# Four strips of array columns for the samples' state products, and PSUM banks of their own

## The chip, the cores and the metric

The kernel runs on one core of a Trainium2 chip. The metric is the device time of one execution in microseconds; the median of several runs is compared. A core has five engines with a queue each: TensorE (PE, with weight loads as PEld), VectorE (DVE), ScalarE (ACT), GpSimd (POOL) and SyncE (SP), which here issues most DMAs. Every queue is worked off in order.

## The reference, cut to what matters

One layer of a decoder trunk for a prompt of 1024 tokens and for eight samples of one token each (`NS = 8`), which share the weights: a combined input projection, gated DeltaNet heads, sliding-window attention, an output mix, and a gated feed-forward part. The change is in what the eight samples do with their carried DeltaNet states, one 128x128 state per sample and head (8 heads):

```python
def _gdn_recurrent(q, k, v, beta, g, S0):
    def step(S, inp):
        q_t, k_t, v_t, b_t, g_t = inp
        S = S * jnp.exp(g_t)[..., None, None]
        delta = (v_t - jnp.einsum('bhk,bhkv->bhv', k_t, S)) * b_t[..., None]
        S = S + jnp.einsum('bhk,bhv->bhkv', k_t, delta)
        return S, jnp.einsum('bhk,bhkv->bhv', q_t, S)
```

and in the stage of the two branches around it:

```python
y_a = _gdn_out(o_a, gdn_gate, lp['gdn_onorm_w']) @ lp['w_gdn_out']
y_b = o_b @ lp['w_swa_out']
mix = (jax.nn.sigmoid(ga) * y_a + jax.nn.sigmoid(gb) * y_b) @ lp['w_o']
```

## The kernel before

The program is one long straight line with stages: conditioning and attention; the DeltaNet heads of the prompt; the **branches**; the output mix, feed-forward part and final norm (`second_half`). The order of instructions on each engine is set when the program is built: each operation has a priority (the order of the Python code, shifted by hand in places), and a planner with a model of costs takes, for each engine, what is ready and has room first. On the chip each queue then keeps that order.

A projection (`project`, lines 152 to 164) multiplies 128 output channels by all 1032 columns (1024 of the prompt, 8 of the samples) in three parts of 384, 384 and 264 columns. Each part is 24 matmuls, three for each of eight slices of the contraction (lines 180 to 182: high half by high half, high by low, low by high), added up in one PSUM bank. `evac` empties the bank. `next_mm` (line 174) takes the PSUM pool of the next part from the list `self.mm` in turn. In the branches that list is `[pmm, pmm, pmf]`: pool `pmm` has two banks under the tag "mm", `pmf` one.

In `branches` the attention output ("b2h"/"b2l") is projected with w_swa_out, one tile of 128 channels after another; DVE empties each part by a product with a gate (line 1256) that a DMA reads back from memory into one of three buffers "sgx" (line 1300). Then the operand is replaced by the DeltaNet output "oa" (`load_part`, lines 1191 and 1192), projected with w_gdn_out, and the two are added and split into halves (lines 1260 to 1266).

Between these projection parts one step of `sample_delta` is emitted at a time, each ending at a `yield`. Its steps: load the eight states of each head (line 1079, on SP); activation; norms of q and k by a matmul against ones, a power on GpSimd, a diagonal on DVE and a spread back over the partitions (`rows_rsqrt`, line 1174, and `rows_spread`, line 1180); `kq` and the table "wide" (line 1104); dots of q and k (line 1109); **the products with the states** (line 1121), for two halves of four heads; a copy out of PSUM by ACT (line 1122); eight transposes (line 1126, recorded under the helper's line 190); the deltas; the output with a second norm; and the update of the states (GpSimd line 1161, DVE line 1163, stores line 1165). The samples' tiles in PSUM all come from `pmm`, tag "mm": they share the two banks with the projections.

"wide" holds, for each head, eight blocks of 16 columns, one for each sample b; block b is zero but for columns 2b and 2b + 1, where k and q of that sample stand. The eight products of a head are thus added up in the same 16 partitions of PSUM, row 2b and 2b + 1 being those of sample b. An f32 matmul is two passes on PE. The modulation (line 264), in the first stage, multiplies in a different way: four products, each with 32 columns of weights, write to partitions 0, 32, 64 and 96 onward, and a second product with "strips" (line 270), which holds four stacked identities, adds the four strips up.

Of the kernel before, what the change touches and what calls it, by code (L numbers as in the profile page):

```python
# [9 lines left out]
F32 = mybir.dt.float32  # L10
F32R = mybir.dt.float32r
# [4 lines left out]
PSUM = bass.MemoryType.PSUM  # L16
DRAM = bass.MemoryType.DRAM

P = 128
NP = 1024  # L20
NS = 8
NT = NP + NS
KC = 8
H = 8
# [16 lines left out]
def bc(ap, dim, n):  # L41

    a = ap.unsqueeze(dim)
    shape = list(a.shape)
    shape[dim] = n
    return a.broadcast_to(shape)


def carver(*rooms):

    used = [0] * len(rooms)

    def small(*shape, r=0):
        n = 1
        for x in shape:
            n *= x
        v = rooms[r][:, used[r]:used[r] + n]
        used[r] += n
        letters = "abcd"[:len(shape)]
        return v.rearrange(f"p ({' '.join(letters)}) -> p {' '.join(letters)}", **dict(zip(letters, shape)))  # L60

    return small


class Step:
# [1003 lines left out]
    def sample_delta(self):  # L1069

        nc, I = self.nc, self.I
        zl, cw = self.zl, self.cw
        a, b, c, d, e = (self.t(self.b1, [P, KC, PARTS[t][1]], f"b1{x}{t}", F32R).bitcast(F32).rearrange("p k n -> p (k n)")
                         for x, t in (("h", 1), ("l", 1), ("h", 2), ("l", 2), ("h", 0)))
        small = carver(d, e)
        S0 = []
        for h in range(H):
            S0.append((a, b, c)[h // 3][:, h % 3 * NP:h % 3 * NP + NP].rearrange("p (b v) -> p b v", b=NS))
            nc.sync.dma_start(S0[h], I["state_gdn_S"][0][:, h].rearrange("b k v -> k b v"))
        act, tmp = small(24, NS), small(24, NS)  # L1080
        nc.vector.tensor_tensor(act, zl[:, :, 3:11], bc(cw[:, 3, :], 2, NS), op=ALU.mult)
        nc.vector.tensor_tensor(act, act, self.gsp, op=ALU.add)
        nc.scalar.activation(tmp, act, AF.Tanh, scale=0.5)
        nc.vector.scalar_tensor_tensor(act, tmp, 1.0, act, op0=ALU.add, op1=ALU.mult)

        flat = lambda a: a.rearrange("p a h b -> p (a h b)")
        f3 = lambda a: a.rearrange("p h b -> p (h b)")
        qk = act[:, 0:16, :].rearrange("p (a h) b -> p a h b", a=2)
        v = act[:, 16:24, :]
        sq = small(2, H, NS)  # L1090
        nc.vector.tensor_tensor(sq, qk, qk, op=ALU.mult)
        wide = small(H, NS, 2 * NS)
        nc.gpsimd.memset(wide, 0.0)
        yield
        ps = self.t(self.pmm, [P, 1], "mm")
        nc.tensor.matmul(ps, flat(sq), self.ones[:, 0:1], start=True, stop=True)
        r = self.rows_rsqrt(small, ps, P, 1.0, 4 * EPS)
        yield
        rl = self.rows_spread(*r).rearrange("p (a h b) -> p a h b", a=2, h=H)
        kq = self.const([P, H, NS, 2], "kq")  # L1100
        nc.vector.tensor_tensor(kq[:, :, :, 0], qk[:, 1], rl[:, 1], op=ALU.mult)
        nc.vector.scalar_tensor_tensor(kq[:, :, :, 1], qk[:, 0], P ** -0.5, rl[:, 0], op0=ALU.mult, op1=ALU.mult)
        for i in range(2):
            nc.vector.tensor_copy(wide.rearrange("p h b c -> p h (b c)")[:, :, i::2 * NS + 2], kq[:, :, :, i])
        yield
        pr = small(H, NS)
        nc.vector.tensor_tensor(pr, kq[:, :, :, 0], kq[:, :, :, 1], op=ALU.mult)
        dots = self.t(self.pmm, [P, H, NS], "mm")
        nc.tensor.matmul(f3(dots), self.ones, f3(pr), start=True, stop=True)
        qkd = small(H, NS)  # L1110
        nc.vector.tensor_copy(qkd, dots)
        yield
        eg = self.egb[:, :, 0, :].rearrange("p b h -> p h b")
        beta = self.egb[:, :, 1, :].rearrange("p b h -> p h b")

        rows = small(H, P, r=1)[:2 * NS]
        for h0 in (0, 4):
            ps = self.t(self.pmm, [2 * NS, 4, P], "mm")
            for h in range(4):
                for b in range(NS):  # L1120
                    nc.tensor.matmul(ps[:, h, :], wide[:, h0 + h, b, :], S0[h0 + h][:, b, :], start=b == 0, stop=b == NS - 1)
            nc.scalar.copy(rows[:, h0:h0 + 4, :], ps)
            yield
        pks = self.t(self.pmm, [P, H, NS, 2], "mm")
        for h in range(H):
            self.transpose(pks[:, h].rearrange("p b a -> p (b a)"), rows[:, h, :])
        yield
        pk, dl, o = small(H, NS, 2), small(H, NS), small(H, NS)
        nc.vector.tensor_tensor(pk, pks, bc(eg, 3, 2), op=ALU.mult)
        nc.vector.tensor_scalar_mul(dl, v, 0.5)  # L1130
        nc.vector.tensor_tensor(dl, dl, pk[:, :, :, 0], op=ALU.subtract)
        nc.vector.tensor_tensor(dl, dl, beta, op=ALU.mult)
        yield
        ps = self.t(self.pmm, [H * NS, P], "mm")
        self.transpose(ps, f3(dl))
        dlT = small(P, r=1)[:H * NS]
        nc.vector.tensor_copy(dlT, ps)
        dlr = self.t(self.dr, [H, NS, P], "dlr")
        nc.sync.dma_start(dlr.rearrange("h b v -> (h b) v"), dlT)
        yield  # L1140
        nc.vector.tensor_tensor(o, qkd, dl, op=ALU.mult)
        nc.vector.tensor_tensor(o, o, pk[:, :, :, 1], op=ALU.add)

        nc.vector.tensor_tensor(pr, o, o, op=ALU.mult)
        yield
        ps = self.t(self.pmm, [H * NS, 1], "mm")
        nc.tensor.matmul(ps, f3(pr), self.ones[:, 0:1], start=True, stop=True)
        r = self.rows_rsqrt(small, ps, H * NS, 1.0 / P, EPS)
        yield
        rl = self.rows_spread(*r).rearrange("p (h b) -> p h b", h=H)  # L1150
        nc.vector.tensor_tensor(o, o, rl, op=ALU.mult)
        nc.vector.scalar_tensor_tensor(o, o, self.onw, self.sgs, op0=ALU.mult, op1=ALU.mult)
        nc.sync.dma_start(self.oa[:, :, NP:NT].rearrange("i p b -> p i b"), o)

        for h in range(H):
            if h % 4 == 0:
                yield
            db = self.t(self.b1, [P, KC, 384], "b1l0", F32R).bitcast(F32).rearrange("p k n -> p (k n)") if h == 0 else db
            d = db[:, h % 3 * NP:h % 3 * NP + NP].rearrange("p (b v) -> p b v", b=NS)
            nc.sync.dma_start(d, dlr[h].unsqueeze(0).broadcast_to([P, NS, P]))  # L1160
            nc.gpsimd.tensor_tensor(d, d, bc(kq[:, h, :, 0], 2, P), op=ALU.mult)
            for b in range(NS):
                nc.vector.scalar_tensor_tensor(S0[h][:, b, :], S0[h][:, b, :], self.egb[:, b, 0, h:h + 1], d[:, b, :],
                                               op0=ALU.mult, op1=ALU.add)
            nc.sync.dma_start(self.O[3][0][:, h].rearrange("b k v -> k b v"), S0[h])
# [10 lines left out]

    def rows_spread(self, dg, n):

        out = self.t(self.pmm, [P, n], "mm")
        self.nc.tensor.matmul(out, self.ones[:n, :], dg[:n, :n], start=True, stop=True)  # L1180
        return out

# [62 lines left out]
    def branches(self, pool, pool2):  # L1245
        nc, I = self.nc, self.I
# [3 lines left out]
        for _ in self.filler:  # L1250
            pass
        samples = self.sample_delta()
        gate = lambda src, j, t: self.gate_part(pool, src[j][:, PARTS[t][0]:PARTS[t][0] + PARTS[t][1]], t)

        def yb_out(t, ps):
# [536 lines left out]
    def run(self):  # L1792
        S, nc = ExitStack, self.nc
# [54 lines left out]
            self.a2 = self.norm_scale(self.const([P, KC, 9], "a2"), 32, self.n2w)  # L1848
        with S() as c:
            pool2, pool = self.pool("p6b", 1, ctx=c), self.pool("p6", 1, ctx=c)  # L1850
            self.branches(pool, pool2)
        cg.close()
        self.wctx.close()
        self.second_half()
# [40 lines left out]
```

## Time and profile before

| | |
|---|---|
| median of 3 runs | 2203.2 us (2201.71 to 2215.32) |
| the profiled execution | 2208.18 us, its span 2206.5 us |
| PE busy / weight loads | 2116.8 us (96%) / 1997.0 us |
| DVE, ACT, POOL busy | 1350.5, 792.4, 298.9 us |
| mean granted clock of PE | 0.967 |

Busy time counts from the start to the modelled end of an instruction, and matmuls overlap, so the length of a block of matmuls is better read from start to start. A clock of 1.00 is full speed. An instruction's line is the line of the kernel at which it was recorded; instructions of a helper carry the helper's line. A releaser is the instruction whose semaphore ended an engine's wait.

### The profile page before, as it was taken

The numbers are of one execution on the slowest core, as the hardware profiler recorded it, in microseconds if no ns is written. First come the engines' busy times: TensorE is split into PE (matmuls) and PEld (weight loads), VectorE is DVE, ScalarE is ACT, GpSimd is POOL, SyncE is SP. The second block draws the span as 40 slices with busy tenths as digits, with TensorE's granted clock in tenths as the row PEclk, the third lists the DMA queues.
The fourth block names the chain that finished last, engine by engine and source line by source line (L and its number), as shares of the span: only waits on it lengthen the run. The fifth ranks groups of instructions, "written<-read, shape, count | busy, mean of one in ns | idle before, by whom it ended". The sixth has DMA issues, their size and how long they took to land.

```text
span 2206.5 us, 41136 instructions
## 1 busy us (share of the span) xinstructions
PE 2116.8 (96%) x16507; PEld 1997.0 (91%) x16507; DVE 1350.5 (61%) x2935; ACT 792.4 (36%) x2010; POOL 298.9 (14%) x395
## 2 busy tenths in 40 slices
PE   7899998999999999999999899999999999999998
PEld 3886876899899998998998899999999999999998
DVE  5756665365555756765323665578776776766565
ACT  3445454333243434334222032344333433432102
POOL 1000000011221210111111300002332332100000
PEclk9999997999999989999999999999999999999999
DMA  9333231142222321221327663622323232363202
GB/s 345 108 107 113 86 129 60 49 132 63 70 79 59 80 64 42 62 65 50 88 75 209 202 188 103 184 64 78 97 73 92 69 96 68 97 220 126 87 3 78
DMA packets 265090, 223.93 MB, mean 101 GB/s; under 512 B 57462, under 2 KB 232473, under 8 KB 264882
## 3 DMA queue, kind: packets, MB, share of 16 engines
q1 hardware_dynamic: 263570, 217.01, 32.3%
q10 hardware_dynamic: 1152, 3.70, 0.4%
q8 instruction: 130, 2.13, 0.4%
q14 instruction: 62, 0.51, 0.1%
q0 software_dynamic: 176, 0.59, 0.1%
HBM read 171.28 MB, written 52.35 MB: 101 GB/s over the span
## 4 chain that ended last, share of the span: by engine, by line
PE 82%; DVE 7%; DMA 5%; ACT 3%; issue 2%; SPq 1%; POOL 1%; DVEq 0%; POOLq 0%; ACTq 0%
PE mm L180 18%; PE mm L182 17%; PE mm L181 17%; PE wv L181 3%; PE wv L182 3%; PE wv L180 3%; PE wy L182 2%; PE wy L180 2%; PE wy L181 2%; PE pt L190 1%; PE pv L648 1%; PE tp L190 1%; PE pv L646 1%; PE mm L264 1%; DMA raw<-in_w_in_dram 1%
## 5 line engine op out<-in xcount | busy, mean ns | idle before, releaser
L180 PE MATMUL mm<-b1h,wh 128*128 128x384 f32 (+1 forms) x1440 | 474.4, 331 | 13.6 <-DVE kl L540 4.7
L181 PE MATMUL mm<-b1l,wh 128*128 128x384 f32 (+1 forms) x1440 | 468.3, 326 | 0.0
L182 PE MATMUL mm<-b1h,wl 128*128 128x384 f32 (+1 forms) x1440 | 466.6, 325 | 1.1 <-DVE wl L130 1.1
L180 PEld LDWEIGHTS mm<-b1h,wh 128*128 128x128 f32 x1440 | 273.7, 190 | 25.5 <-issue 6.2
L182 PEld LDWEIGHTS mm<-b1h,wl 128*128 128x128 f32 x1440 | 273.2, 190 | 7.2 <-issue 4.0
L181 PEld LDWEIGHTS mm<-b1l,wh 128*128 128x128 f32 x1440 | 274.2, 191 | 4.1 <-issue 3.6
L129 ACT ACTIVATE wh<-raw 128x1024 fp32r<-128x1024 f32 x77 | 80.7, 1048 | 178.8 <-PE mm L181 128.7
L130 DVE TENSOR_TENSOR wl<-raw,wh 128x1024 fp32r<-128x1024 f32 x76 | 95.9, 1261 | 72.5 <-ACT wh L129 71.4
L180 PE MATMUL mm<-b2h,wh 128*128 128x384 f32 (+1 forms) x384 | 124.2, 324 | 2.5 <-DVE t L1256 2.1
L180 PE MATMUL mm<-pk,w 128*128 128x260 f32 (+1 forms) x440 | 124.6, 283 | 2.0 <-ACT r L1534 1.4
L181 PE MATMUL mm<-pk,w 128*128 128x260 f32 (+1 forms) x440 | 124.4, 283 | 0.8 <-DVE pk L130 0.8
L182 PE MATMUL mm<-pk,w 128*128 128x260 f32 (+1 forms) x440 | 124.3, 283 | 0.0
L181 PE MATMUL mm<-b2l,wh 128*128 128x384 f32 (+1 forms) x384 | 123.4, 321 | 0.0
L182 PE MATMUL mm<-b2h,wl 128*128 128x384 f32 (+1 forms) x384 | 122.6, 321 | 0.4 <-DVE wl L130 0.4
L182 PE MATMUL mm<-bmh,pk 128*128 128x256 f32 (+1 forms) x380 | 108.9, 287 | 0.7 <-DVE pk L130 0.7
L180 PE MATMUL mm<-bmh,pk 128*128 128x260 f32 (+1 forms) x380 | 108.8, 286 | 0.6 <-ACT pk L129 0.6
L1378 DVE SCALAR_TENSOR_TENSOR x<-mm,mT,x 128x256 f32<-128x256 f32 (+2 forms) x133 | 63.6, 482 | 70.4 <-PE mm L182 70.1
L181 PE MATMUL mm<-bml,pk 128*128 128x260 f32 (+1 forms) x353 | 100.8, 285 | 0.0
L180 PE MATMUL mm<-bmh,w 128*128 128x260 f32 (+1 forms) x320 | 90.9, 284 | 0.0
L182 PE MATMUL mm<-bmh,w 128*128 128x260 f32 (+1 forms) x320 | 90.8, 284 | 0.0
L130 DVE TENSOR_TENSOR w<-ws,w 128x512 fp32r<-128x512 f32 x88 | 60.2, 685 | 41.7 <-ACT w L129 41.7
L180 PEld LDWEIGHTS mm<-pk,w 128*128 128x128 f32 x440 | 82.9, 188 | 2.6 <-ACT r L1534 1.6
(596 smaller groups left out, 5724.0 us busy)
## 6 DMA issues: line engine op xcount, KB each, us to landing
raw<-in_w_in_dram SPq DMA_DIRECT2D x60, 512.0 KB
bml<-act SPq DMA_DIRECT2D x22, 516.0 KB
raw<-in_w_ffn_gate_dram SPq DMA_DIRECT2D x22, 512.0 KB
raw<-in_w_ffn_up_dram SPq DMA_DIRECT2D x22, 512.0 KB
raw<-in_w_ffn_down_dram SPq DMA_DIRECT2D x22, 512.0 KB
qst<-in_w_mod_dram SPq DMA_DIRECT2D x16, 512.0 KB
raw<-in_w_mod_dram SPq DMA_DIRECT2D x16, 512.0 KB
act<-fa SPq DMA_DIRECT2D x22, 260.0 KB
```

The source lines that it names most:

```text
L129: self.nc.scalar.activation(hi, x, AF.Copy)
L130: (eng or self.nc.vector).tensor_tensor(lo, x, hi.bitcast(F32), op=ALU.subtract)
L180: mm(ps, whi, xhi, start=first, stop=False, **kw)
L181: mm(ps, whi, xlo, start=False, stop=False, **kw)
L182: mm(ps, wlo, xhi, start=False, stop=last, **kw)
L190: self.nc.tensor.transpose(out, in_, self.ident[:p, :p])
L264: nc.tensor.matmul(ps[32 * j:32 * j + 32], self.cT[:, k0 + j, :], ws[j // 2][:, j % 2, :], start=k0 == 0, stop=k0 > 0)
L646: nc.tensor.matmul(out, V[:, n, ch], pc[:, r::2, :], start=True, stop=n == 0)
L648: nc.tensor.matmul(out, V[:, n - 1, ch], pp[:, r::2, :], start=False, stop=True)
L1378: nc.vector.scalar_tensor_tensor(x[:, :np_], ps[:, :np_], self.mT[:, m + j, 8:9], x[:, :np_], op0=ALU.mult, op1=ALU.add)
```

## The change

Three things change, all for the branches.

- "wide" has blocks of 32 columns in place of 16, and lies in a buffer that was free (the one that the broadcast deltas use afterwards). The product of sample b goes to the PSUM partitions from 32 (b % 4) on, so samples 0 to 3 open four strips and 4 to 7 add to them. The copy out of PSUM then takes 128 partitions where it took 16, and the eight transposes become eight plain matmuls against "fold", four stacked identities of 16 columns, which add up the strips.
- The samples' PSUM tiles come from a new pool `pso`, tag "sm", of two banks.
- The projections of the branches take turns on four banks: two of `pmm` and two of `pso` (tag "mm"); `pmf` is left out there. Before the second half the list is set back to `[pmm, pmm, pmf]`.

```diff
-        wide = small(H, NS, 2 * NS)
+        wide = self.t(self.b1, [P, KC, 384], "b1l0", F32R).bitcast(F32).rearrange("p k n -> p (k n)")
+        wide = wide[:, :H * NS * 32].rearrange("p (h b c) -> p h b c", h=H, b=NS)
         nc.gpsimd.memset(wide, 0.0)
+        fold = small(2 * NS, r=1)
+        for j in range(4):
+            r = slice(32 * j, 32 * j + 32)
+            nc.gpsimd.tensor_copy(fold[r], self.ident[r, 32 * j:32 * j + 2 * NS])
...
-        ps = self.t(self.pmm, [P, 1], "mm")
+        ps = self.t(self.pso, [P, 1], "sm")
...
-            nc.vector.tensor_copy(wide.rearrange("p h b c -> p h (b c)")[:, :, i::2 * NS + 2], kq[:, :, :, i])
+            nc.vector.tensor_copy(wide.rearrange("p h b c -> p h (b c)")[:, :, i::34], kq[:, :, :, i])
...
-        rows = small(H, P, r=1)[:2 * NS]
+        rows = small(H, P, r=1)
         for h0 in (0, 4):
-            ps = self.t(self.pmm, [2 * NS, 4, P], "mm")
+            ps = self.t(self.pso, [P, 4, P], "sm")
             for h in range(4):
                 for b in range(NS):
-                    nc.tensor.matmul(ps[:, h, :], wide[:, h0 + h, b, :], S0[h0 + h][:, b, :], start=b == 0, stop=b == NS - 1)
+                    r = slice(32 * (b % 4), 32 * (b % 4) + 32)
+                    nc.tensor.matmul(ps[r, h, :], wide[:, h0 + h, b, :], S0[h0 + h][:, b, :], start=b < 4, stop=b > 3)
             nc.scalar.copy(rows[:, h0:h0 + 4, :], ps)
             yield
-        pks = self.t(self.pmm, [P, H, NS, 2], "mm")
+        pks = self.t(self.pso, [P, H, NS, 2], "sm")
         for h in range(H):
-            self.transpose(pks[:, h].rearrange("p b a -> p (b a)"), rows[:, h, :])
+            nc.tensor.matmul(pks[:, h].rearrange("p b a -> p (b a)"), rows[:, h, :], fold, start=True, stop=True)
...
     def rows_spread(self, dg, n):
-        out = self.t(self.pmm, [P, n], "mm")
+        out = self.t(self.pso, [P, n], "sm")
...
         samples = self.sample_delta()
+        self.mm = [self.pmm, self.pmm, self.pso, self.pso]
...
             pool2, pool = self.pool("p6b", 1, ctx=c), self.pool("p6", 1, ctx=c)
+            self.pso = self.pool("q6", 2, PSUM, ctx=c)
             self.branches(pool, pool2)
+        self.mm = [self.pmm, self.pmm, self.pmf]
```

The other tiles of `sample_delta` in PSUM (dots, the deltas' transpose, the second norm) move from `pmm` to `pso` in the same way.

More of the change, by code (lines that the diff above doesn't have):

```diff
@@ L1107, in sample_delta @@
         nc.vector.tensor_tensor(pr, kq[:, :, :, 0], kq[:, :, :, 1], op=ALU.mult)
-        dots = self.t(self.pmm, [P, H, NS], "mm")
+        dots = self.t(self.pso, [P, H, NS], "sm")
         nc.tensor.matmul(f3(dots), self.ones, f3(pr), start=True, stop=True)
@@ L1133, in sample_delta @@
         yield
-        ps = self.t(self.pmm, [H * NS, P], "mm")
+        ps = self.t(self.pso, [H * NS, P], "sm")
         self.transpose(ps, f3(dl))
@@ L1145, in sample_delta @@
         yield
-        ps = self.t(self.pmm, [H * NS, 1], "mm")
+        ps = self.t(self.pso, [H * NS, 1], "sm")
         nc.tensor.matmul(ps, f3(pr), self.ones[:, 0:1], start=True, stop=True)
```

## The prediction

> **What bounds the kernel now.** I read the page's busy shares first, then the windows around the stage that the change touches, then the waits of TensorE (PE) there, then the timeline at each wait.
>
> ```profile
> PE 2116.8 (96%) x16507; PEld 1997.0 (91%) x16507; DVE 1350.5 (61%) x2935; ACT 792.4 (36%) x2010; POOL 298.9 (14%) x395
> ```
>
> PE is busy in 96% of the span: what shortens PE's own work, or an idle gap of PE, counts; what another engine saves does not. The change sits in the branches, the stage of the two output projections. The columns of a window are the stretch, its length, then busy us (instructions) of PE, weight loads, VectorE (DVE), ScalarE, GpSimd, then granted clock, DMA share, GB/s.
>
> ```profile
> 1168.00:1261.00 93.00, 83.02 (x535) 78.92 (x534) 38.94 (x92) 8.07 (x11) 15.85 (x10) 0.93 0.63 177
> ```
>
> In the 93 us in which the samples are woven in, PE is idle for 10 us and runs at 0.93 of its clock. The waits of PE from 1160 to 1420 us (total us, times, longest) say for whom:
>
> ```profile
> PE mm L1180 <- DVE b1h L1174: 3.8, 1, 3.8
> PE mm L1180 <- DVE t L1256: 2.8, 1, 2.8
> PE mm L180 <- DVE t L1256: 2.1, 1, 2.1
> ```
>
> Two are waits for L1256, which empties a projection's PSUM bank: bank waits. The first is a wait for data. The timeline at the first bank wait (start, us, engine; in brackets idle time and releaser):
>
> ```profile
> 1176.65 3.37 SPq L1079 DMA_DIRECT2D b1h<-in_state_gdn_S_dram  x2
> 1180.06 2.01 SPq L1300 DMA_DIRECT2D sgx<-sgb  x1
> ```
>
> ```profile
> 1176.37 0.29 DVE L1174 TENSOR_SCALAR b1h<-ident,b1h 128x128 f32<-128x128 f32 x1 [0.71 <-POOL b1h L125]
> 1186.28 0.43 DVE L1256 TENSOR_TENSOR t<-mm,sgx 128x264 f32<-128x264 f32 x1 [9.63 <-DMA sgx<-sgb]
> ```
>
> ```profile
> 1186.77 0.80 PE L1180 MATMUL mm<-b1h,ones 128*128 128x128 f32 x2 [2.84 <-DVE t L1256]
> 1188.47 0.66 PE L1109 MATMUL mm<-b1l,ones 128*128 128x64 f32 x2 [0.90 <-DVE b1l L1107]
> 1189.45 0.59 PE L180 MATMUL mm<-b2h,wh 128*128 128x264 f32 x1 [0.32 <-DVE b1l L1111]
> ```
>
> The gate tile sgx is queued on SP behind the loads of the states; its landing frees L1256, that frees a bank of the pool "mm", and only then can the samples' spread L1180 write, although its own input (L1174) was ready at 1176.7. The three projection banks are all full by then. I call this **gap A**: 2.8 + 0.9 + 0.3 = 4.1 us of idling. **Gap B** is the second spread:
>
> ```profile
> 1235.72 5.99 DVE L1163 SCALAR_TENSOR_TENSOR b1h<-b1h,egb,b1l 128x128 f32<-128x128 f32 x8 [2.81 <-POOL b1l L1161]
> ...
> 1244.60 0.24 DVE L1174 TENSOR_SCALAR b1h<-ident,b1h 64x64 f32<-64x64 f32 x1
> ```
>
> ```profile
> 1244.90 0.69 PE L1180 MATMUL mm<-b1h,ones 64*128 64x64 f32 x2 [3.78 <-DVE b1h L1174]
> 1247.73 0.59 PE L180 MATMUL mm<-b2h,wh 128*128 128x264 f32 x1 [2.14 <-DVE t L1256]
> ```
>
> DVE is in the state updates L1163; both the diagonal L1174 and the emptying of two full projections stand behind them. Each gap also drops the clock:
>
> ```profile
> 1189.40:1194.30 4.90, 4.85 (x24) 4.76 (x24) 2.06 (x3) 0.00 (x0) 0.00 (x0) 0.59 0.52 151
> ...
> 1217.80:1220.80 3.00, 3.00 (x27) 2.97 (x26) 1.60 (x7) 0.00 (x0) 0.00 (x0) 1.00 0.24 66
> ...
> 1247.70:1252.40 4.70, 4.67 (x24) 4.67 (x25) 2.58 (x10) 0.00 (x0) 1.91 (x1) 0.60 1.11 353
> ```
>
> One 264-column projection (24 matmuls) takes 3.0 us at full clock, 4.9 after gap A and 4.7 after gap B: 1.9 and 1.7 us more.
>
> **Part 1: the products with the states on four strips.** In the chain by time, each half of L1121 (four heads) is 64 passes of PE, and nothing runs beside them:
>
> ```profile
> 1194.42 7.09 PE mm L1121 x64
> ...
> 1205.89 7.09 PE mm L1121 x64
> ```
>
> 14.2 us in all, 0.111 us a pass, all on the strip of array columns 0 to 31. The change gives sample b the strip b % 4. The number of passes stays 128 (32 columns of weights where there were 16), so all depends on whether passes on different strips overlap. The modulation's products (L264) are built in this way, with 512 moving columns:
>
> ```profile
> 135.38 0.62 PE L264 MATMUL mm<-wmh,cTr 128*32 128x512 f32 x1
> 135.38 0.62 PE L264 MATMUL mm<-wml,cTr 128*32 128x512 f32 x2
> 135.40 0.62 PE L264 MATMUL mm<-raw,cTr 128*32 128x512 f32 x1
> 135.83 0.59 PE L264 MATMUL mm<-wmh,cTr 128*32 128x512 f32 x1
> 135.84 0.60 PE L264 MATMUL mm<-wml,cTr 128*32 128x512 f32 x2
> 135.85 1.44 PE L264 MATMUL mm<-raw,cTr 128*32 128x512 f32 x7
> 137.22 0.44 PE L181 MATMUL mm<-b1l,wh 128*128 128x384 f32 x1
> ```
>
> Four passes start within 0.02 us, the next four 0.45 us later; 14 passes, in waves of four, four, three and three, need 1.84 us until the next work starts, 0.46 a wave. That is what one pass of four times 128 columns needs (4 x 0.111 = 0.44). So a wave of four 128-column passes should take 0.111 us, and a half 16 x 0.111 = 1.8, with 0.2 to fill 2.0: 4.0 for both, **10.2 us saved**. Ends: no overlap saves nothing, 32 perfect waves (3.5) save 10.7.
>
> Do the weight loads hide when a wave is only 0.111 us long? In the modulation the second set of weights loads while the first wave runs:
>
> ```profile
> 135.42 0.11 PEld L264 LDWEIGHTS mm<-raw,cTr 128*32 128x32 f32 x1
> ```
>
> This load starts at 135.42, inside the wave that began at 135.38, and lasts as long as a short wave. The Trainium skill, "TensorE: Matmul & The Clock Gate", Part 3, The mechanism, says the opposite for this case: LDWEIGHTS overlaps with matmuls in flight "only when row_grp differs", and all strips here use all rows. By that rule the loads of each wave would stand in the open; the row speaks against it. What such loads in the open would cost is a rival below.
>
> **Part 2: the transposes become products with "fold".** Eight transposes are replaced by eight plain f32 products of two passes each, with 128x128 weights and 16 moving columns. The nearest row is the modulation's L270 (9 columns), eight passes:
>
> ```profile
> 142.63 1.06 PE L270 MATMUL mm<-strips,mrows 128*128 128x9 f32 x8
> ```
>
> ```profile
> 1217.27 0.67 PE L190 MATMUL mm<-ident,b1h 16*128 16x16 f32 x8
> ```
>
> 16 passes at 1.06 / 8 = 0.13 are 2.1 us, against 0.7 now: **1.4 us more** (at the transposes' own 0.084 a pass, 0.7 more).
>
> **Part 3: the banks.** The samples get two banks ("sm"), the projections four instead of three, shared with no one. In gap A, L1180 no longer waits for L1256: 2.8 us, the 0.3 behind it, and the 1.9 of slow clock go. The 0.9 in which L1109 waits for its operand on DVE I leave in. **5.0 us saved** (ends 0 and 6.0). What is late next there: with a fourth bank PE may run one more projection (3.0 us) from 1183.9, and the bank of the gate tile's projection is free at 1186.7, so no new wait follows.
>
> Gap B is worth 3.8 + 2.1 + 1.7 = 7.6 us on PE: two full projections need not stop a third and a fourth one. But here something else is nearly as late. The DMA in the stretch behind it:
>
> ```profile
> 1235.00:1245.00 10.00, 6.22 (x37) 5.90 (x35) 9.28 (x18) 0.00 (x0) 4.98 (x4) 0.98 0.40 115
> ...
> 1250.00:1285.00 35.00, 35.00 (x223) 35.00 (x222) 25.42 (x57) 6.59 (x8) 9.20 (x5) 0.98 0.99 308
> ```
>
> ```profile
> 1271.20 0.39 SPq L1165 DMA_DIRECT2D out_dram<-b1h  x1
> ...
> 1273.40 2.01 SPq L1191 DMA_DIRECT2D b2l<-oa  x4
> ...
> 1280.33 1.91 SPq L1191 DMA_DIRECT2D b2l<-oa  x4
> ```
>
> From 1250 to 1285 the DMA is busy at 0.99 (state stores, broadcasts of the deltas, then the next operand oa). The first load of oa is issued 2.2 us after the last state store, so a PE that is 7.6 us earlier meets the same stores and waits for oa. Between 0 and 7.6 I take **3 us**, near what those two issues leave.
>
> **At nothing:** GpSimd's memset of "wide" doubles and four small copies for fold are added. They stand at 1164, some 12 us ahead of the moment (1176.4) at which L1174 is released by GpSimd's power L125, and "wide" is not read before the products at 1194; without that cover they would cost about their length.
>
> ```profile
> L1093 POOL MEMSET b1l<- x1: 962/962/962, 1164.0 to 1164.0; 128x1024 f32 x1
> ```
>
> So some 1 us, and the copies, at worst. ScalarE's two copies out of PSUM keep 512 elements a partition. No DMA is added and none moves to another queue. "wide" now takes the room that the broadcast of the deltas takes after it; the products have read it before the deltas exist.
>
> **Sum.** -10.2 + 1.4 - 5.0 - 3.0 = -16.8 us. The profiled execution took 2208.2 us (span 2206.5 and 1.7 around it) and would take 2191.4. It was 5.0 above the median of 2203.2, so for the median I take 2186.4.
>
> **The rivals.**
>
> 1. *The order keeps the waits.* PE works through its queue in order, and that order is planned. If the dots L1109 come to stand ahead of a projection while DVE's queue still has L1256 with its late gate tile ahead of L1107, PE waits until about 1188 all the same, now for data, and a fourth bank is of no use. Gaps A and B stay; only -10.2 + 1.4 = -8.8: 2194.4. If L1109 stands a whole projection earlier, up to 4.4 us more idling (384 columns, 3.0 x 384 / 264): 2198.8. For it: L1109 waited for DVE already (0.90). Against: L1180's input was there 10 us before it ran, so it can move up, and DVE was idle for 9.63 us in which L1101 to L1107 would fit.
> 2. *All gaps close:* -10.2 + 1.4 - 6.0 - 7.6 = -22.4: 2180.8. Against it the DMA share of 0.99.
> 3. *The weight loads of the strips do not hide:* each wave costs a load and a pass, 0.11 + 0.111; 32 waves are 7.1, and with 0.4 to fill the saving is 6.7 instead of 10.2: 2189.9. This is the rule named above. The row of 135.42 is against it.
> 4. *The strips are no use and slow each other (slower):* a change of strip lets the array run empty, so that every pass costs its whole recorded length, not its spacing.
>
> ```profile
> L1121 PE MATMUL mm<-b1h,b1l x80: 272/273/283, 1194.3 to 1212.7; 128*16 128x128 f32 x80
> ```
>
> 128 x 0.273 = 34.9 us, 20.7 more; with the rest of the sum (+1.4 - 8.0) 14.1 more than before: 2217.3. It decides from 0.163 us a pass on. L264, which changes strips at every product, is against it.
>
> **Chances.** Forecast 0.58, rival 1 0.21, rival 2 0.12, rival 3 0.05, rival 4 0.04. The range goes from below rival 2 to above rival 1's worst, with some 2 to 5 us for how far three runs scatter here: 2175 to 2201. One per cent, 22 us (2181.2 and 2225.2), is about what a measurement of this kernel can tell from no change. All terms together hardly reach it: faster 0.16 (rival 2 and the low edge of the forecast), same 0.81, slower 0.03.
>
> **What the changed profile would show.** L1121's halves as blocks of about 2 us, four passes starting together; if 7 us, the strips do not overlap, and at 3.5 the loads are in the open. The fold products as 16 passes in about 2 us. L1180 with no idle time for L1256 before it, and PE's clock at 1.0 behind. Around the second L1180 a projection running before it. ScalarE's first split of oa, and the weights of the next stage behind it, waiting longer for DMA if gap B is given back there. The prediction is wrong if a new order puts PE behind DVE at another place, or if the second half, which is planned anew, gains or loses by itself: I count nothing for it.

## The result, and the profile after

The change brought **2203.2 us (9 runs, 2201.71 to 2218.89) down to 2190.1 us (9 runs, 2182.88 to 2196.09)**; the ratio of the times is 0.9918, with a 95% interval from 0.9893 to 0.9944. That is inside the forecast range and 3.7 us above the forecast of 2186.4. The profiled execution took 2194.39 us with a span of 2192.6 us, against the forecast 2191.4. One execution of the kernel before, in the session of the first experiments, took 5977.32 us and counts in no ratio. The page's line of busy time and the same 93 us of the branches as in the prediction:

```profile
PE 2102.4 (96%) x16515; PEld 1984.6 (91%) x16515; DVE 1348.5 (62%) x2935; ACT 792.7 (36%) x2010; POOL 302.1 (14%) x399
```

```profile
1168.00:1261.00 93.00, 87.59 (x661) 85.35 (x660) 44.73 (x112) 9.79 (x11) 17.64 (x10) 1.00 0.79 227
```

PE is idle for 5.4 us of this stretch where it was idle for 10, and its clock is 1.00 where it was 0.93. Lines of the changed kernel behind the table "wide" are numbered 5 to 7 higher: the products are L1127, the second diagonal and spread L1180 and L1186, the emptying of a projection L1263.

To read the stage by itself, without what the rest of the execution did, I take the first start of the first emptying (L1256, after: L1263) and the last start of the last one (L1260, after: L1267). These are the rows by line, before and then after (x24 each; the two numbers behind the durations are the first and last start):

```profile
L1256 DVE TENSOR_TENSOR t<-mm,sgx x24: 422/546/558, 1170.8 to 1288.6; 128x384 f32<-128x384 f32 x16, 128x264 f32<-128x264 f32 x8
...
L1260 DVE TENSOR_TENSOR sgx<-mm,sgx x24: 432/557/558, 1293.2 to 1376.8; 128x384 f32<-128x384 f32 x16, 128x264 f32<-128x264 f32 x8
```

```profile
L1263 DVE TENSOR_TENSOR t<-mm,sgx x24: 423/544/558, 1167.2 to 1268.8; 128x384 f32<-128x384 f32 x16, 128x264 f32<-128x264 f32 x8
...
L1267 DVE TENSOR_TENSOR sgx<-mm,sgx x24: 432/557/558, 1273.6 to 1358.5; 128x384 f32<-128x384 f32 x16, 128x264 f32<-128x264 f32 x8
```

The **branches** took 206.0 us (1376.8 - 1170.8) and now take 191.3: **14.7 us less**. The stretch ahead of them, in which both kernels run the same instructions, was 3.6 us shorter in this execution (1167.2 against 1170.8), and the rest behind them 4.4 us longer (2192.6 - 1358.5 = 834.1 against 829.7). The three add up to the spans' difference of 13.9.

**The products.** The chain by time has the second half in one piece, and the fold products in another; the rows by line give the weight loads; the timeline gives the first half from its start to the next projection:

```profile
1190.73 1.88 PE sm L1127 x64
...
1196.99 1.69 PE sm L1132 x16
```

```profile
L1127 PEld LDWEIGHTS sm<-b1h,b1l x80: 106/110/110, 1183.8 to 1192.2; 128*32 128x32 f32 x80
```

```profile
1183.76 1.52 PE L1127 MATMUL sm<-b1h,b1l 128*32 128x128 f32 x48
1185.09 0.62 PE L1127 MATMUL sm<-b1l,b1l 128*32 128x128 f32 x16
1185.64 0.45 PE L180 MATMUL mm<-b2h,wh 128*128 128x384 f32 x1
```

Each half takes 1.88 us, from 7.09: 10.4 us less for the two. The 64 weight loads of a half last 0.11 us each, 7.0 us in sum, and lie inside those 1.88 us. The fold products take 1.69 us, about 1.0 more than the transposes.

**Gap A** is gone. The timeline of PE and of DVE there, and the clock:

```profile
1176.50 0.38 PE L1186 MATMUL sm<-b1h,ones 128*128 128x128 f32 x2
...
1180.89 0.33 PE L1114 MATMUL sm<-b1l,ones 128*128 128x64 f32 x2
```

```profile
1176.92 0.22 DVE L1106 TENSOR_TENSOR kq<-b1l,sm 128x64 f32<-128x64 f32 x1 [3.72 <-PE sm L1186]
...
1182.45 0.43 DVE L1263 TENSOR_TENSOR t<-mm,sgx 128x264 f32<-128x264 f32 x1 [4.82 <-DMA sgx<-sgb]
```

```profile
1183.90:1189.40 5.50, 5.13 (x82) 4.61 (x78) 2.50 (x4) 1.64 (x2) 0.00 (x0) 1.00 0.46 134
1189.40:1194.30 4.90, 4.90 (x82) 4.45 (x81) 1.69 (x2) 1.65 (x2) 0.00 (x0) 1.00 0.31 102
```

The spread L1186 runs in the middle of a projection, without waiting, and the samples' steps on DVE from L1106 on run at 1176.92, ahead of the emptying that waits for its gate tile, in idle time. So the dots L1114 find their operand ready as well, and the clock stays at 1.00 (0.59 before).

**Gap B** changed its shape. The waits of PE from 1160 to 1420 us:

```profile
PE mm L180 <- ACT wh L129: 3.0, 2, 1.8
PE sm L1186 <- DVE b1h L1180: 2.6, 1, 2.6
...
PE mm L180 <- ACT pk L129: 1.7, 1, 1.7
PE mm L182 <- DVE wl L130: 1.6, 3, 0.6
```

The bank wait of 2.1 us is gone, and the wait for the diagonal is 2.6 in place of 3.8. In their place PE waits 3.0 + 1.6 us for weights (wh, wl) a little later, and behind the last of them the clock falls (timeline, then window):

```profile
1245.13 0.45 PE L180 MATMUL mm<-b2h,wh 128*128 128x384 f32 x1 [1.75 <-ACT wh L129]
...
1265.90 0.45 PE L180 MATMUL mm<-b2h,wh 128*128 128x384 f32 x1 [1.28 <-ACT wh L129]
...
1267.16 0.44 PE L182 MATMUL mm<-b2h,wl 128*128 128x384 f32 x1 [0.64 <-DVE wl L130]
```

```profile
1267.00:1273.20 6.20, 6.04 (x25) 6.04 (x26) 3.85 (x6) 2.85 (x5) 0.00 (x0) 0.72 0.78 246
```

How much of the gain is there before gap B begins, an emptying behind the products shows, the tenth of the stage before and after, 19.35 us earlier:

```profile
1225.24 0.56 DVE L1256 TENSOR_TENSOR t<-mm,sgx 128x384 f32<-128x384 f32 x1 [1.96 <-PE mm L182]
```

```profile
1205.89 0.56 DVE L1263 TENSOR_TENSOR t<-mm,sgx 128x384 f32<-128x384 f32 x1 [1.96 <-PE mm L182]
```

Less the 3.6 us from before the branches that is 15.7 us of gain up to there: 10.4 from the products, less 1.0 for fold, and so, as the remainder, **6.3 from gap A**. At the end of the branches 14.7 us are left: the part with gap B did not gain 3, it **lost 1.0**.

### The profile page after: what moved, and what is told of

Same layout as the page of the kernel before. It is cut to its first block, busy times and chain, and to the rows that moved or that the text cites. A ratio compares the mean times of both kernels' runs of the same rounds, so it can differ in the third digit from the quotient of the medians.

```text
span 2192.6 us, 41162 instructions
## 1 busy us (share of the span) xinstructions
PE 2102.4 (96%) x16515; PEld 1984.6 (91%) x16515; DVE 1348.5 (62%) x2935; ACT 792.7 (36%) x2010; POOL 302.1 (14%) x399
## 4 chain that ended last, share of the span: by engine, by line
PE 80%; DVE 7%; DMA 5%; ACT 3%; SPq 2%; issue 2%; POOL 1%; DVEq 0%; POOLq 0%; ACTq 0%
PE mm L180 17%; PE mm L182 17%; PE mm L181 17%; PE wv L181 3%; PE wv L180 3%; PE wv L182 3%; PE wy L182 2%; PE wy L180 2%; PE wy L181 2%; PE pt L190 1%; PE pv L648 1%; PE pv L646 1%; PE tp L190 1%; PE mm L264 1%; ACT osq L846 1%
## 5 line engine op out<-in xcount | busy, mean ns | idle before, releaser
L180 PE MATMUL mm<-b1h,wh 128*128 128x384 f32 (+1 forms) x1440 | 473.1, 330 | 14.4 <-DVE kl L540 4.7
L180 PEld LDWEIGHTS mm<-b1h,wh 128*128 128x128 f32 x1440 | 272.9, 190 | 26.7 <-issue 6.2
L130 DVE TENSOR_TENSOR wl<-raw,wh 128x1024 fp32r<-128x1024 f32 x76 | 93.4, 1230 | 73.9 <-ACT wh L129 72.9
L180 PE MATMUL mm<-pk,w 128*128 128x260 f32 (+1 forms) x440 | 124.7, 284 | 2.0 <-ACT r L1541 1.4
L180 PE MATMUL mm<-b2h,wh 128*128 128x384 f32 (+1 forms) x384 | 123.6, 322 | 3.0 <-ACT wh L129 3.0
L180 PE MATMUL mm<-bmh,pk 128*128 128x260 f32 (+1 forms) x380 | 109.7, 289 | 1.7 <-ACT pk L129 1.7
L180 PE MATMUL mm<-bmh,w 128*128 128x260 f32 (+1 forms) x320 | 91.1, 285 | 0.0
L130 DVE TENSOR_TENSOR w<-ws,w 128x512 fp32r<-128x512 f32 x88 | 60.3, 686 | 41.7 <-ACT w L129 41.7
L180 PEld LDWEIGHTS mm<-pk,w 128*128 128x128 f32 x440 | 82.9, 188 | 2.6 <-ACT r L1541 1.6
```

What stands on the lines that cost most here:

```text
L130: (eng or self.nc.vector).tensor_tensor(lo, x, hi.bitcast(F32), op=ALU.subtract)
L180: mm(ps, whi, xhi, start=first, stop=False, **kw)
```

## The experiments

The scatter of a single execution (mostly within 10 us of the median, once 15.7) is as large as the effects, so each kernel is judged by two numbers: the ratio of its times to those of the kernel before, and the length of the branches in its profile, read from the same two rows as above. The branches' length is of one execution, but it leaves out the scatter of the rest. Each edit is planned anew, so the order on the queues can move with it. The diffs are against the changed kernel, where nothing else is said.

| kernel | median us (runs) | ratio, 95% interval | branches us | against before |
|---|---|---|---|---|
| before | 2203.2 (9) | | 206.0 | |
| the change | 2190.1 (9) | 0.9918 (0.9893 to 0.9944) | 191.3 | -14.7 |
| the change again | 2187.56 (6) | 0.9914 (0.9883 to 0.9944) | 191.8 | -14.2 |
| strips alone | 2196.72 (8) | 0.9955 (0.9930 to 0.9980) | 195.7 | -10.3 |
| both bank edits alone | 2199.52 (12) | 0.9972 (0.9954 to 0.9990) | 200.4 | -5.6 |
| own banks alone | 2201.0 (12) | 0.9973 (0.9955 to 0.9991) | 198.9 | -7.1 |
| four banks, shared, alone | 2206.13 (12) | 1.0013 (0.9998 to 1.0028) | 203.5 | -2.5 |
| strips and own banks | 2189.47 (7) | 0.9931 (0.9908 to 0.9955) | 191.4 | -14.6 |
| two strips | 2195.63 (1) | | 194.9 | -11.1 |
| strip by strip | 2195.08 (1) | | 191.5 | -14.5 |
| small state store | 2189.92 (4) | 0.9931 (0.9904 to 0.9958) | 195.7 | -10.3 |
| state stores on ACT | 2200.04 (12) | 0.9978 (0.9964 to 0.9992) | 198.0 | -8.0 |
| diagonal on GpSimd | 2192.15 (6) | 0.9941 (0.9922 to 0.9959) | 191.2 | -14.8 |
| both of these | 2201.25 (12) | 0.9980 (0.9966 to 0.9995) | 197.5 | -8.5 |

**The change again.** The same kernel, to see what of its profile recurs.

> The changed kernel itself once more, for a second profile. In its first profile the stretch ahead of the branches was 3.5 us earlier than before although its instructions are the same, and the output pass lost 4.3 us to one late tile of w_o (1.7 us of idling and a slow clock behind it). If both are chance of one execution, this profile shows other values: ahead of the branches within 3 us of before's 1167.6 (end of the last gate), and no wait over 1 us for the weights of the output pass. If they belong to the change, both come again. Time: 2186 to 2191 by either.

Branches 191.8 us, and the rest behind them 829.9 us (2191.3 - 1361.4), as in the kernel before (829.7). So the 4.4 us that the first profile of the change lost behind the branches did not come again. The loss at gap B did: the tenth emptying starts 38.8 us after the first (38.7 in the first profile), and the whole stage is 14.2 us shorter, 1.4 less than the 15.6 gained up to there. In that profile a weight tile of the output projection came late (the wait of 1.7 us for "pk" in the list above). Over all profiles below, this rest is between 828.0 and 834.2 us long.

**Strips alone**: the samples' tiles back in `pmm`, the projections on three banks.

```diff
-            ps = self.t(self.pso, [P, 4, P], "sm")
+            ps = self.t(self.pmm, [P, 4, P], "mm")
...
-        self.mm = [self.pmm, self.pmm, self.pso, self.pso]
```

> Strips and fold as in the change; the samples share the two banks of the projections' pool again, and the projections take turns on three banks. If PE's own time is taken off one for one: -10.4 for the products, +1.2 for fold, both gaps as before, 2194 (2191 to 2197). If the strips only pay where the banks let the chain of the samples run ahead, the gain turns into longer bank waits: 2199 or more.

The time is 0.45% less, about 9.9 us. The waits of PE from 1160 to 1300 us are the old ones, with nearly the old lengths:

```profile
PE mm L1186 <- DVE b1h L1180: 3.4, 1, 3.4
PE mm L1186 <- DVE t L1262: 2.7, 1, 2.7
PE mm L180 <- DVE t L1262: 2.1, 1, 2.1
```

The strips shorten PE's own work and touch no wait.

**Both bank edits alone** (products, "wide" and transposes as before):

```diff
-                    r = slice(32 * (b % 4), 32 * (b % 4) + 32)
-                    nc.tensor.matmul(ps[r, h, :], wide[:, h0 + h, b, :], S0[h0 + h][:, b, :], start=b < 4, stop=b > 3)
+                    nc.tensor.matmul(ps[:, h, :], wide[:, h0 + h, b, :], S0[h0 + h][:, b, :], start=b == 0, stop=b == NS - 1)
```

> Banks as in the change (two of the samples' own, four for the projections); products on one strip, 16 columns, with transposes. If gap A closes and gap B is given back to DMA, as the changed profile shows: -6.7 + 1.1, 2197.6 (2195 to 2200), and the timeline shows no idle time of PE for the evacuations. If the banks only pay with the strips: 2203. If the banks are the main thing: 2192 or less.

About 6.2 us by the ratio, 5.6 by the branches, and PE waits for no emptying from 1160 to 1300 us, as expected.

**Own banks alone.** Is it the sharing that held PE, or the number of the projections' banks? The kernel just shown, but the projections stay on their three banks:

```diff
-        self.mm = [self.pmm, self.pmm, self.pso, self.pso]
```

> Only the samples' two banks: products on one strip, projections on three banks in turn. If the three full projection banks are what holds PE in gap A, PE still waits about 2.5 us for the late evacuation, now in a projection: half of gap A, 2200 (2198 to 2202). If it is the sharing that holds PE, this alone closes gap A: 2197.6, like the banks together.

About 6.0 us by the ratio, as much as with the fourth bank. PE's timeline at gap A:

```profile
1183.49 0.33 PE L1109 MATMUL sm<-b1l,ones 128*128 128x64 f32 x2
1183.75 2.14 PE L1121 MATMUL sm<-b1h,b1l 128*16 128x128 f32 x18
1185.94 0.39 PE L180 MATMUL mm<-b2h,wh 128*128 128x264 f32 x1
...
1189.04 3.45 PE L1121 MATMUL sm<-b1h,b1l 128*16 128x128 f32 x30
```

While the three projection banks are full, PE does 18 passes of the products; it is the samples' own work that fills the time. I had expected a projection to stand waiting there, and that half of the gap would stay.

**Four banks, shared, alone**: the reverse, the samples in `pmm` as before the change, and the projections on four banks. Against the kernel before:

```diff
+            self.pso = self.pool("q6", 2, PSUM, ctx=c)
...
+        self.mm = [self.pmm, self.pmm, self.pso, self.pso]
```

> The kernel before with four banks for the projections, the samples sharing two of them as before, products on one strip: the last of the four combinations of the bank edits. If the sharing is what holds PE, a fourth bank brings little: gap A stays at 2.8 us or more of waiting for L1256 and the time is 2202 to 2204. If a fourth bank is worth as much as the samples' own two: 2198 to 2200.

No gain by the ratio; the branches of the one profile are 2.5 us shorter. The expectation had the time right for a wrong reason: the banks are still shared, and yet the bank wait of gap A is gone. The waits of PE from 1160 to 1300 us say what stands in its place:

```profile
PE mm L180 <- ACT wh L129: 5.2, 4, 1.7
PE mm L1180 <- DVE b1h L1174: 1.8, 1, 1.8
PE mm L182 <- DVE wl L130: 1.6, 3, 0.6
```

Two of them, 1.70 us for wh and 0.61 us for wl, stand at 1189 and 1190 us, where gap A was. A fourth bank lets the projections run ahead, up to the next missing weights.

**Strips and own banks**: the change without the fourth bank (the same one line removed as above).

> The change without the fourth bank: strips, fold and the samples' own two banks, projections on three banks in turn. Since the own banks alone gave as much as both bank edits, the same as the change: 2188 (2185 to 2191). If the fourth bank counts as soon as the products are short (they filled the time in which three banks were full when they were long): 2 to 3 us more, 2191, with an idle time of PE ahead of a projection for an evacuation.

The ratio and the branches (191.4 us) are those of the change. The fourth bank adds nothing to it that these runs can tell. Its place is seen in the waits all the same: without it, PE waits 2.3 us for emptyings (L180 for DVE's L1262) and 2.3 us for weights from 1160 to 1300 us, where the change waits for weights alone, 4.6 us.

**Two strips**, r = 32 (b % 2), and **strip by strip**, with the loop `for b in (0, 4, 1, 5, 2, 6, 3, 7)`, so that the two samples of one strip follow each other:

> The changed kernel with the samples on two strips (b % 2) in place of four. If strips overlap and nothing else makes the products short, a half of 64 passes takes 32 waves of 0.111 and some 0.2, 3.7 us, between the 7.1 of one strip and the 1.9 of four. If the weights' width, the new bank or the order made them short, it stays at 1.9.

> The changed kernel with samples in the order 0, 4, 1, 5, 2, 6, 3, 7, so that two products (four passes) of one strip follow one another. If PE starts passes strictly in order, a strip's later passes hold up the next strip: about 13 waves per head in place of 4, 5.6 us a half. If it starts passes of other strips past one that waits for its strip, a half stays at 1.9 to 2.2.

Each ran once. With two strips the copy out of PSUM and fold take 64 partitions. PE's timeline, first halves, of the one and of the other, each with the projection behind it:

```profile
1184.53 2.81 PE L1127 MATMUL sm<-b1h,b1l 128*32 128x128 f32 x48
...
1188.14 0.45 PE L180 MATMUL mm<-b2h,wh 128*128 128x384 f32 x1
```

```profile
1189.16 1.57 PE L1127 MATMUL sm<-b1h,b1l 128*32 128x128 f32 x48
...
1191.12 0.44 PE L180 MATMUL mm<-b2h,wh 128*128 128x384 f32 x1
```

Two strips: 3.61 us a half, close to half of 7.09, and branches 3.6 us longer than the change's, which is twice the difference of the halves (2 x 1.73 = 3.5). Strip by strip: 1.96 us, as good as the order by waves.

**Small state store.** My reason for counting only 3 us at gap B was the full DMA. Here only sample 0's states are stored (samples 1 to 7 of that output are left out), an eighth of the bytes:

```diff
-            nc.sync.dma_start(self.O[3][0][:, h].rearrange("b k v -> k b v"), S0[h])
+            nc.sync.dma_start(self.O[3][0][0:1, h].rearrange("b k v -> k b v"), S0[h][:, 0:1, :])
```

> The changed kernel, storing only sample 0 of each head's new states (the states of samples 1 to 7 are left out of the output): the same DMAs, in the same queue with the same waits for DVE, with an eighth of the bytes. If gap B's gain is given back to DMA bandwidth, the waits of PE for weights between the state updates and the second projection (ACT wh and DVE wl, 3 to 4 us in the changed kernel) fall below 1 us and the kernel gains some 4 us: 2184. If the order of the queues holds the weights back, the waits stay and the time stays at 2188.

The window from 1225 to 1245 us of the change, then of this kernel (the last columns are granted clock, DMA share and GB/s), and this kernel's waits of PE from 1160 to 1300 us:

```profile
1225.00:1245.00 20.00, 18.25 (x116) 17.86 (x116) 14.81 (x45) 2.04 (x2) 8.45 (x4) 1.00 1.03 306
```

```profile
1225.00:1245.00 20.00, 17.66 (x108) 16.89 (x107) 18.22 (x42) 2.12 (x2) 9.66 (x5) 0.98 0.59 179
```

```profile
PE mm L180 <- ACT wh L129: 3.2, 2, 1.6
PE mm L180 <- DVE t L1263: 2.5, 1, 2.5
PE sm L1186 <- DVE b1h L1180: 2.5, 1, 2.5
```

The DMA share fell from 1.03 to 0.59, and PE still waits 1.64 us for the weights for which it waits 1.75 us in the change; a bank wait came back, and the branches are 4.4 us longer than the change's (the ratio tells no difference). **Fewer bytes alone do not bring gap B's gain back.** But this run does not clear the DMA, for its order is another one. In the change, 32 of DVE's state updates stand ahead of the split L130 that frees the buffer of the raw weights; here it is 40. SP's load of the next weights goes out as soon as that split ends, at 1237.89:

```profile
1234.97 0.32 SPq L1166 DMA_DIRECT2D b1l<-dlr  x1
...
1237.92 0.38 SPq L135 DMA_DIRECT2D raw<-in_w_swa_out_dram  x1
```

What the stores cost in the order of the change is read from the change's own rows, in the section on the prediction.

**State stores on ScalarE's queue** (to take them out of SP's queue, where each waits for DVE's updates), **the diagonal on GpSimd** (to take it from behind DVE's updates), and **both**:

```diff
-            nc.sync.dma_start(self.O[3][0][:, h].rearrange("b k v -> k b v"), S0[h])
+            nc.scalar.dma_start(self.O[3][0][:, h].rearrange("b k v -> k b v"), S0[h])
```

```diff
-        nc.vector.tensor_scalar_mul(dg[:n, :n], self.ident[:n, :n], r[:n, 1:2])
+        nc.gpsimd.tensor_scalar_mul(dg[:n, :n], self.ident[:n, :n], r[:n, 1:2])
```

> The changed kernel with the eight stores of the new states issued by ScalarE's queue in place of SP's. With an eighth of the bytes stored, the DMA was busy at 0.6 and PE still waited for the weights, so bandwidth is not what eats gap B's gain. If it is SP's queue, which waits 12 us for DVE's state updates ahead of these stores while weights and operands are queued behind, the waits of PE for weights there (3 to 4 us) fall below 1.5 us and the time to some 2185. If the wait only moves to ScalarE, whose splits of the weights now stand behind the stores, or if DVE itself is the limit: 2188 or more.

> The changed kernel with the diagonal of the norms (the DVE instruction that the second spread waits for, 2.5 us of PE) computed by GpSimd right behind its power. If that wait is a loss of its own, it goes and the time is 2185 to 2186. If the stretch up to the second projection is bound by DVE's updates and the queues, PE waits as much more for weights there, and the time stays at 2188.

> Both edits on the changed kernel: 2182 to 2183 if the two waits add up; 2185 to 2188 if one takes the place of the other.

The first is some 10 us slower than the change by the medians, 6.7 of it in the branches: PE waits 6.4 us for wh there, 4.6 of them at once at 1274. The second took the whole wait for the diagonal away and has the change's branches (191.2 us) all the same. Its waits of PE from 1160 to 1300 us:

```profile
PE mm L180 <- ACT wh L129: 6.0, 2, 4.9
```

The waits for wl come to 0.7 us beside these. So the 2.6 us of waiting for the diagonal reappear as 2.1 us more of waiting for weights (6.7 in place of 4.6). Both together are as slow as the first (197.5 us in the branches).

**Where in the stage each edit acts.** The tenth emptying (the rows at 1225.24 and 1205.89 us above) splits the branches into a part with the products and gap A and a part with gap B. One profile each, in us:

| kernel | banks of the projections | first to tenth emptying | from there to the last |
|---|---|---|---|
| before | 3 | 54.4 | 151.6 |
| strips alone | 3 | 44.9 | 150.8 |
| own banks alone | 3 | 47.7 | 151.2 |
| strips and own banks | 3 | 40.2 | 151.2 |
| four banks, shared, alone | 4 | 51.3 | 152.2 |
| both bank edits alone | 4 | 47.5 | 152.9 |
| the change | 4 | 38.7 | 152.6 |
| the change again | 4 | 38.8 | 153.0 |

The first part gains from the strips and from the own banks. The second hardly moves, and where it is longer than before, the projections have four banks: so it is too with two strips, strip by strip and the diagonal on GpSimd (152.5 to 153.0). The three kernels with changed stores, which have four banks as well, took 156.9 to 158.6 us there.

## Why the prediction was right, step by step

- **Strips: -10.2 forecast, -10.4 measured**, and 9.9 by the ratio of the strips alone. The wave of four passes in 0.111 us, taken from the modulation's rows, holds: 16 waves in 1.88 us. Rivals 3 and 4 are out: loads in the open would have made a half 3.5 us, and rival 4 17.5. The rule of the Trainium skill that I set against the row ("TensorE: Matmul & The Clock Gate", Part 3, The mechanism: loads overlap with matmuls only where the row group differs) does not describe this: 7.0 us of loads, all on the same rows, lie within 1.88 us.
- **Fold: +1.4 forecast, +1.0 measured.** A pass is 0.106 us (1.69 / 16), not the 0.13 of L270.
- **Gap A: -5.0 forecast, -6.3 measured.** The waits and the slow clock that the term added up are gone. The 0.9 us that I left in went too, because DVE's steps moved ahead of the emptying that waits for its gate tile. This is the opposite of rival 1, which is out. Most of the price belongs to the samples' own banks, to judge by the first part of the stage: 4.7 us with the strips and 6.7 without. The fourth bank brought 1.5 and 0.2 there.
- **Gap B: -3.0 forecast, +1.0 measured.** This is the term that failed. I put the gap at 3.8 + 2.1 + 1.7 = 7.6 us and expected 4.6 of them back, as waiting for oa behind a full DMA. The changed profile has 2.64 us of waiting for the diagonal, 1.75 + 0.64 and 1.28 + 0.64 us of waiting for weights and, from the 0.72 over 6.2 us, some 1.7 us of slow clock: 8.7 us. Three things in it differ:

  The 3.8 us were a wait for data, as my own reading of the list says, and I counted them as if banks could close them. The diagonal stands behind DVE's updates as before; 1.1 us went.

  The wait of 1.28 + 0.64 us at 1266 is of the kind that I forecast. ScalarE splits the next weights, a tile of w_gdn_out, only behind its splits of oa, and these wait for DMA:

```profile
1264.06 0.85 ACT L129 ACTIVATE b2h<-b2l 128x768 fp32r<-128x768 f32 x1 [1.71 <-DMA b2l<-oa]
1264.81 1.04 ACT L129 ACTIVATE wh<-raw 128x1024 fp32r<-128x1024 f32 x1
```

  The first new wait, for a tile of w_swa_out, I had not looked for at all. What the trace of the change shows there, on SP, DVE and ACT in turn:

```profile
1235.03 2.61 SPq L1166 DMA_DIRECT2D b1l<-dlr  x1
...
1238.21 0.38 SPq L135 DMA_DIRECT2D raw<-in_w_swa_out_dram  x1
```

```profile
1233.04 1.22 DVE L130 TENSOR_TENSOR wl<-raw,wh 128x1024 fp32r<-128x1024 f32 x1
1236.22 3.84 DVE L1169 SCALAR_TENSOR_TENSOR b1l<-b1l,egb,b1l 128x128 f32<-128x128 f32 x8 [1.96 <-POOL b1l L1167]
```

```profile
1244.02 1.06 ACT L129 ACTIVATE wh<-raw 128x1024 fp32r<-128x1024 f32 x1 [12.76 <-DMA raw<-in_w_swa_out_dram]
```

  DVE has read the buffer of raw weights at 1234.26, and the next weights could be loaded into it. SP issues that load only at 1238.21, behind the broadcast of a delta and a gate tile in its queue; it lands at 1244.02, and PE has waited 1.75 us when the split weights are there. So the stretch is tied to a chain in which SP's queue, the states' updates on DVE and one raw buffer stand in order. The stores seem to lengthen it: with them ahead in SP's queue, the issue of a delta's broadcast takes 0.52 to 2.61 us of SP from 1222 on, and 0.32 each time in the two kernels that store an eighth or store from ScalarE's queue. The load takes 5.8 us from issue to split, and 4.65 in the kernel that stores an eighth. An estimate from these rows is that the stores cost this chain 2.3 + 1.2 = 3.5 us; what PE would gain by it was not shown, as both kernels have another order.

  Removing a wait of PE just ahead of the chain lets PE reach the next missing weights sooner. The diagonal on GpSimd shows this exchange, and so does the fourth bank: with it the second part of the stage is 1.4 us longer in the kernels with strips and 1.7 us without, while the own banks, with three for the projections, left it 0.4 us shorter than before. Which link of the chain holds the others I could not show: taking the stores out of SP's queue made the stage longer.
- **Sum: -16.8 forecast, -14.7 in the branches** (-14.2 in the second profile). The errors of the four terms, -0.2, -0.4, -1.3 and +4.0, make 2.1. They cancel in part, which is luck. So is a part of the nearness of the medians: I took off the 5.0 us by which the profiled execution before lay above its median, and the profiled execution after happens to lie 4.3 us above its own. Rival 2, in which all gaps close, was not reached because of gap B. By the ratio the change is worth 18 us, with an interval from 12 to 24 that holds both. By the ratios the edits add up (strips 9.9 and own banks 6.0 are 15.9); by the branches not quite (10.3 and 7.1, against 14.6 for the two together).
- **At nothing:** the memset and the copies on GpSimd, and the larger copy out of PSUM, show no wait, as forecast. For the second half I counted nothing, and the second profile of the change (829.9 us against 829.7) bears that out.

## What to carry to other kernels

Where a short serial chain is woven into a stream of matmuls, look at whose PSUM banks it shares: two banks of its own were worth 6 us here, and one more bank for all of them nothing that the times can tell. The price of an unfamiliar form (strips, a fold) is best taken from another place in the same kernel that already uses it; two such rows gave the strips' gain to 0.2 us and fold's cost to 0.4. An idle gap of PE that stands just ahead of a chain of loads and updates counts at nothing until something shows that the chain itself is early.

## What the runs showed that I had not expected

- **The order of the strips does not matter.** With one strip a pass needs 0.111 us, so the order strip by strip, each pass started behind the one before it in the program, should take 12 x 0.111 = 1.3 us a head and over 5 us a half; it took 1.96 us. In the built program PE's instructions do stand in this order. The change's own order has the same in small: the two passes of a product are on one strip, so that starting strictly in order a half should take 32 x 0.111 = 3.6 us, not 1.88. Passes must overlap with others than their neighbours in the program; the records do not say which strip a pass was on.
- **Executions of the same instructions differ by up to 11.6 us before the branches begin.** The first emptying started between 1164.4 us (small state store) and 1176.0 us (strips and own banks), with the same instructions up to there. These two ran on the same chip; what makes the difference was not tried. The branches alone agree to 0.5 us between the two profiles of the change. A stage's own length, between two landmarks in it, told the edits apart where single times of the whole did not.
- **The same gap is followed by different clocks.** The change's first profile has 2.64 us of waiting for the diagonal, its second profile 2.49 us at the same place. The 4 us behind it, in the one and in the other (the clock is the last number but two):

```profile
1225.10:1229.10 4.00, 3.97 (x28) 3.91 (x29) 3.27 (x11) 0.00 (x0) 0.78 (x1) 1.00 1.00 272
```

```profile
1227.40:1231.40 4.00, 3.95 (x22) 3.88 (x23) 3.29 (x11) 0.00 (x0) 0.39 (x1) 0.73 1.03 267
```

  In strips and own banks 2.52 us were followed by 0.57. The 1.28 and 0.64 us around 1266 were followed by 0.72 over the next 6.2 us. So the length of a gap of this size does not tell whether a slow clock follows, and the 1.9 and 1.7 us of slow clock that the prediction read from one profile are values of that execution.
